# One joint inverse for the blocks of four heads, a pool of SBUF for the opening, and modulation's products joined by fours and by twos

## The chip, the cores and the metric

The kernel runs on one core of a Trainium2 chip. The metric is device time in microseconds (us), as the median of three runs. The engines are named as the profile names them: PE is TensorE, PEld its weight loads, DVE is VectorE, ACT is ScalarE, POOL is GpSimd and SP is SyncE, which here issues all DMAs. Matrix products of the type float32r (here two halves of a float32, high and low) pass the array once, products of plain float32 are recorded as two instructions each.

## The reference

The reference is a decoder trunk of two layers on 256 tokens of width 2048, in float32. Each layer computes

```
mod = silu(c) @ w_ada[l] + b_ada[l]        # 2048 x 12288; six vectors: shift, scale, gate, twice
h = rms_norm(x) * (1 + scale) + shift
proj = h @ w_in[l]                         # q,k,v,z of 8 DeltaNet heads, 16 query heads, 2 k, 2 v
x = x + gate * (concat(deltanet, attention) @ w_out[l])
h = rms_norm(x) * (1 + scale') + shift'
x = x + gate' * ((silu(h @ w_gate) * (h @ w_up)) @ w_down)
```

For this change the DeltaNet head matters. After a causal convolution of four taps and a silu, q and k are normalised; per head there is a matrix of scores of k against k with a decay, and the reference solves with its lower triangle:

```
lower = where(strict, (k beta) k^T * decay, 0) + eye
t_inv = triangular_solve(lower, eye)       # the inverse, per chunk of 64 tokens
w, u = t_inv @ (k beta exp(g)), t_inv @ (v beta)
```

## The kernel before

The program is written through a planner. Each piece of work is a Python generator that yields the engine of its next step; a class `Timed` keeps a clock of estimated costs for each engine, and `Steps` lets a piece go on when that clock says that its input is there. So the order of instructions on each engine is fixed when the program is built; on the chip, semaphores hold each instruction until its input is there. All DMAs stand in one order on SP, and a DMA that waits for a free buffer holds those behind it.

The program runs in these stages: an **opening**, the rest of layer 0's **heads** stage, layer 0's **FFN** stage, layer 1's heads stage, layer 1's FFN stage. In the FFN stages and in the projections, each weight block of 128x128 is split by ACT and DVE (or POOL) into a high half `wh` and a low half `wl`; for one block PE computes `wh` with both halves of the activation `act` and `wl` with its high half. In the heads stages these are three products of 256 columns, in the FFN stages one of 512 columns and one of 256. Weights come in loads of 512 KB through 4 buffers `w`.

In the opening, w_ada for two of the six vectors of layer 0 (64 loads of 512 KB, tile `wada`, 3 buffers, class `Ada`) is multiplied on PE (`products`): one load gives four matmuls of 32x256 in plain float32, which stand in the four column groups of the array. Another 64 such loads follow in layer 0's heads stage; all other w_ada rows go to DVE. As soon as columns of the modulation are there, the activations `hs` are made one after another, and 28 of the 42 column tiles of w_in (`EARLY`) are multiplied in groups of k (`GROUPS`), the last of which, k from 10 on, begins the heads stage.

The list `JOBS` sets the order of the 42 projections: for head after head k, q, one pair of attention queries (aq), v, z. `delta` is one DeltaNet head from k and q to its output. It computes the matrix `B` of scores, then inverts the diagonal blocks of 16x16 of its triangle, one head at a time: DVE masks and sums the blocks into `mc` (128x2x16), spreads them into `R` (128x512), PE multiplies `R` by a 0/1 matrix (`same`), and on DVE 30 instructions of multiply and sum (`jk`, `uc`) make one column after another. From these blocks, `U` (and its transpose `W`), PE and DVE build the inverse of 128x128 in steps of 16, 32 and 64, and then the output. Before the projection v of head h, the planner waits until `delta` of head h-2 has passed the point "mid".

The main loop projects in the order of `JOBS`; `split_act` takes one of 38 buffers `act`. The wait before v reads `while h > 1 and "mid" not in sts[h - 2]: S.wait()`.

Of the kernel before, what the change touches and what calls it, by code (L numbers as in the profile page):

```python
# [21 lines left out]
F32R = mybir.dt.float32r  # L22
# [7 lines left out]
EPS = 1e-6  # L30
NACT = 38
# [3 lines left out]
AHEAD = 2  # L35
# [25 lines left out]
for _n, _w in (  # L61
    ("ident", 128), ("triX", 256), ("sel", 8), ("ls", 128), ("amask", 256), ("cos", 256), ("sin", 256),
    ("own", 128), ("same", 128), ("id16", 16), ("nid16", 16), ("bm", 8), ("m16", 8),
):
    CONST.add(_n, _w)
# [7 lines left out]
def constants():  # L73
# [10 lines left out]
    out["own"], out["same"], out["bm"] = b16 & (p < j), b16, b16[:, ::16]  # L84
    out["id16"] = p % 16 == np.arange(16)[None, :]
    out["nid16"] = -1.0 * out["id16"]
# [9 lines left out]
class Timed:  # L96
# [13 lines left out]
    def dma(self, out, in_, after=0):  # L110
# [6 lines left out]
        return self.loads + 2000  # L117

# [55 lines left out]
HEADS = {"pm": 3, "psm": 5}  # L174
FFN = {"pr": 2, "psm": 4}


class Build:


    def __init__(self, nc, sb, tc):
        self.nc, self.sb, self.tc = nc, sb, tc
        self.k = self.stage = 0
        self.ps = None
        self.free = {"act": NACT, "cv": 4, "w3": 5, "do": 2, "th": 2, "dn": 2, "ry": 2, "kq": 3, "z": 3, "n2": 6}
# [3 lines left out]
    def banks(self, tags):  # L189

        if self.ps is not None:
            for tag in self.tags:
                assert self.free.pop(tag) == self.total.pop(tag), tag
            self.ps.__exit__(None, None, None)
        self.tags = tags
        if tags:
            self.ps = self.tc.tile_pool(name=f"ps{self.stage}", bufs=1, space=PSUM)
            self.pool = self.ps.__enter__()
            self.stage += 1
            self.free.update(tags)  # L200
            self.total.update(tags)
# [11 lines left out]
    def t(self, tag, shape, dt=F32, bufs=None):  # L213
        self.k += 1
        return self.sb.tile(shape, dt, tag=tag, name=f"{tag}_{self.k}", bufs=self.total.get(tag, bufs))
# [78 lines left out]
class Weights:  # L294
# [6 lines left out]
    def __init__(self, b):  # L301
# [3 lines left out]
        self.tiles, self.freed, self.ready, self.cur = {}, {}, {}, []  # L305

# [23 lines left out]

    def load(self, upto):
        while self.loaded < min(upto, len(self.units), self.loaded - len(self.tiles) + self.BUFS):
            u = self.loaded
            src, n = self.units[u]
            w = self.b.t("w", [128, 1024], bufs=self.BUFS)
# [3 lines left out]
            self.tiles[u] = (w, self.nc.dma(to, src, self.freed.get(u - self.BUFS, 0)))  # L339
# [50 lines left out]
def trunk(tc, xT, bada, c, c_col, par, con, w_in, w_ba, w_ada0, w_ada, w_out, w_gu, w_dn, out):  # L390
    nc = Timed(tc.nc)
    with (
# [4 lines left out]
        b.banks(HEADS)  # L397
# [65 lines left out]
        class Ada:  # L463
            BUFS = 3

            def __init__(self):

                self.todo = [(0, m, j, i) for j in range(8) for m in (1, 0) for i in range(4)]
                self.todo += [(0, m, j, i) for m in COLS[2:] for j in range(8) for i in range(4)]
# [23 lines left out]

            def load(self):
                l, m, k, i = self.todo[self.nload]
                w = b.t("wada", [128, 1024], bufs=self.BUFS)
# [4 lines left out]
                self.tiles[self.nload] = (w, nc.dma(w, src, self.freed.get(self.nload - self.BUFS, 0)))  # L501
                self.nload += 1

            def products(self):
# [3 lines left out]
                for n in range(self.cols):  # L508
# [94 lines left out]
            def loads(self, u):  # L603
                n = min(max(self.want(u + 3), self.force), len(self.todo))
                while self.nload < n and self.nload - self.ndone < self.BUFS:
                    self.load()
# [33 lines left out]
        def pump():  # L640
            while first:
                kind, n = first[0]
                if kind == 0 and ada.nload - ada.ndone < ada.BUFS:
                    ada.load()
                elif kind == 1 and len(W.tiles) < W.BUFS:
# [84 lines left out]
        def act_tile():  # L730
            return b.t("act", [128, 2, T], F32R)

        def split_act(src, outs, at):
            yield from b.take("act", A_)
            a = act_tile()
# [897 lines left out]
```

## Time and profile before

| what | value |
|---|---|
| median of three runs | 2598.65 us |
| fastest and slowest of the three | 2586.24 and 2600.52 us |
| profiled execution, its own time | 2599.8 us |
| its span from first to last instruction | 2598.1 us |
| mean granted TensorE clock | 0.988 |
| busy share of the span: PE, DVE, ACT, POOL | 96%, 73%, 50%, 17% |
| DMA, mean over the span | 234 GB/s |

The time outside the span is 1.7 us. In the page, a group's row gives engine, operation, the tile that is written and the tiles that are read, the shape, the count, the busy time in us, the mean of one in ns, and after the second bar the idle time just before these instructions and what ended it. All rows have the line of the recording helper (L161, and L116 for DMAs), so tiles tell the groups apart.

### The profile page before, as it was taken

The numbers are of one execution on the slowest core, as the hardware profiler recorded it, in microseconds if no ns is written. First come the engines' busy times: TensorE is split into PE (matmuls) and PEld (weight loads), VectorE is DVE, ScalarE is ACT, GpSimd is POOL, SyncE is SP. The second block draws the span as 40 slices with busy tenths as digits, with TensorE's granted clock in tenths as the row PEclk, the third lists the DMA queues.
The fourth block names the chain that finished last, engine by engine and source line by source line (L and its number), as shares of the span: only waits on it lengthen the run. The fifth ranks groups of instructions, "written<-read, shape, count | busy, mean of one in ns | idle before, by whom it ended". The sixth has DMA issues, their size and how long they took to land.

```text
span 2598.1 us, 46969 instructions
## 1 busy us (share of the span) xinstructions
PE 2494.3 (96%) x16910; PEld 2165.7 (83%) x16910; DVE 1905.9 (73%) x4750; ACT 1293.2 (50%) x2760; POOL 440.6 (17%) x391
## 2 busy tenths in 40 slices
PE   6999999898999999999998999999899999999998
PEld 4776777787888888888888898999788888888887
DVE  3656776998777899999997767785877655555565
ACT  3335554335455444555445655544555544555553
POOL 1323333571000000000004434346000000000000
PEclk9999999999999999999998999999999999999999
DMA  8998565686777999999993333356677766555564
GB/s 292 314 331 273 183 209 174 212 294 197 247 256 254 322 346 358 351 352 351 333 334 124 117 121 123 122 171 215 214 258 245 241 187 185 187 189 186 181 187 136
DMA packets 184092, 608.68 MB, mean 234 GB/s; under 512 B 19121, under 2 KB 30513, under 8 KB 183857
## 3 DMA queue, kind: packets, MB, share of 16 engines
q1 hardware_dynamic: 183858, 605.68, 68.8%
q8 instruction: 132, 2.16, 0.3%
q14 instruction: 102, 0.84, 0.1%
HBM read 603.51 MB, written 2.10 MB: 233 GB/s over the span
## 4 chain that ended last, share of the span: by engine, by line
PE 50%; issue 31%; DVE 10%; DMA 5%; ACT 1%; POOL 0%; SPq 0%; DVEq 0%; POOLq 0%; ACTq 0%
PE psm L161 19%; PE pr L161 17%; PE pm L161 14%; DMA wada<-w_ada 5%; DVE wl L161 2%; DVE wada L161 1%; DVE cv L161 1%; ACT wh L161 1%; DVE jk L161 1%; DVE x L161 1%; DVE U L161 0%; DVE R L161 0%; DVE act L161 0%; DVE mc L161 0%; SPq L116 0%
## 5 line engine op out<-in xcount | busy, mean ns | idle before, releaser
L161 ACT CAST wh<-w 128x512 fp32r<-128x512 f32 (+1 forms) x1566 | 913.4, 605 | 471.0 <-PE psm L161 177.0
L161 DVE TENSOR_TENSOR wl<-w,wh 128x512 fp32r<-128x512 f32 (+1 forms) x1301 | 873.0, 687 | 250.7 <-ACT wh L161 240.0
L161 PE MATMUL pr<-act,wh 128*128 128x512 f32 x2816 | 991.5, 397 | 7.3 <-DVE kq L161 4.0
L161 PE MATMUL pr<-act,wl 128*128 128x256 f32 x2816 | 790.2, 281 | 0.0
L161 PE MATMUL pm<-act,wh 128*128 128x256 f32 x3328 | 654.2, 295 | 14.6 <-DVE z L161 5.1
L161 PEld LDWEIGHTS pr<-act,wh 128*128 128x128 f32 x2816 | 530.9, 189 | 135.5 <-DVE act L161 4.7
L161 POOL TENSOR_TENSOR wl<-w,wh 128x512 fp32r<-128x512 f32 (+1 forms) x265 | 366.3, 1390 | 1247.5 <-ACT wh L161 1166.6
L161 PE MATMUL psm<-act,wh 128*128 128x512 f32 (+1 forms) x1792 | 571.9, 375 | 3.2 <-DVE act L161 2.9
L161 PEld LDWEIGHTS pm<-act,wh 128*128 128x128 f32 x3328 | 523.2, 194 | 57.7 <-issue 35.4
L161 PEld LDWEIGHTS pr<-act,wl 128*128 128x128 f32 x2816 | 533.9, 190 | 0.0
L161 PE MATMUL pm<-act,wl 128*128 128x256 f32 x1664 | 473.7, 285 | 0.0
L161 PE MATMUL psm<-act,wl 128*128 128x256 f32 x1600 | 449.0, 281 | 0.0
L161 DVE CUSTOM_DVE_ANT_0 wada<-wada,cs 128x1024 f32<-128x1024 f32 x256 | 329.0, 1286 | 97.4 <-DMA wada<-w_ada 97.0
L161 PEld LDWEIGHTS psm<-act,wh 128*128 128x128 f32 x1792 | 325.0, 189 | 81.0 <-issue 10.7
L161 PEld LDWEIGHTS pm<-act,wl 128*128 128x128 f32 x1664 | 321.8, 193 | 0.0
L161 PEld LDWEIGHTS psm<-act,wl 128*128 128x128 f32 x1600 | 303.5, 190 | 0.0
L161 ACT COPY kq<-pr 128x512 f32<-128x512 f32 x88 | 51.6, 587 | 179.5 <-PE pr L161 179.4
L161 POOL TENSOR_TENSOR n2r<-ms,halfc 128x2 f32<-128x2 f32 x5 | 3.4, 689 | 810.5 <-DVE ms L161 810.5
L161 DVE TENSOR_TENSOR kq<-pr,kq 128x512 f32<-128x512 f32 x88 | 60.5, 688 | 75.7 <-ACT kq L161 75.7
L161 PE MATMUL psm<-wada,cs 128*32 128x256 f32 x1024 | 87.6, 416 | 28.3 <-DMA wada<-w_ada 28.1
L161 DVE SCALAR_TENSOR_TENSOR x<-psm,mod,x 128x256 f32<-128x256 f32 x128 | 61.9, 483 | 62.7 <-PE psm L161 60.3
L161 ACT ACTIVATE th<-kq 128x256 f32<-128x256 f32 x88 | 36.8, 418 | 76.4 <-DVE kq L161 76.4
(176 smaller groups left out, 1723.9 us busy)
## 6 DMA issues: line engine op xcount, KB each, us to landing
wada<-w_ada SPq DMA_DIRECT2D x384, 512.0 KB, 5.8
w<-w_gu SPq DMA_DIRECT2D x352, 512.0 KB, 4.9
w<-w_in SPq DMA_DIRECT2D x147, 512.0 KB, 3.8
w<-w_dn SPq DMA_DIRECT2D x128, 512.0 KB, 4.6
w<-w_out SPq DMA_DIRECT2D x64, 512.0 KB, 3.8
w<-w_dn SPq DMA_DIRECT2D x64, 384.0 KB, 4.4
w<-w_in SPq DMA_DIRECT2D x28, 384.0 KB, 4.7
x<-xT SPq DMA_DIRECT2D x4, 512.0 KB, 7.6
```

The source lines that it names most:

```text
L161: return f(*a, **k)
```

## The change

The inverses of the 16x16 blocks are made for four heads at once. `delta` is cut in two: `scores` goes as far as `mc` of its head; when four heads are there, `inverses` runs once. It carries `mc` by eight small DMAs (8 KB each) into `qi`, where one partition holds a whole 16x16 block, so that the inverse is made along the free dimension: blocks of 2, then 4, 8 and 16 with 18 to 20 DVE instructions on 64 partitions for all four heads. Eight more DMAs carry the result back into `uc`. The 0/1 product and `R` of before are gone, and so are the 30 instructions per head. `delta` then starts from `uc`; the transposes of v move from its start to after the inverse, and "mid" with them; the sum of squares of q moves into `scores`.

`JOBS` now has k and q of heads 0 to 3 first, then v, z of head h with k, q, aq of head h+4 behind them.

SBUF gets pools by stage. The opening has its own: 8 buffers `wx` for the first 64 loads of w_ada instead of 3, and 4 buffers `wy` for every second load of w_in beside the 4 of `w`. The heads stages get `B` six times instead of twice in the freed room; 8 of the 38 `act` buffers become `mid`, for the FFN stage alone.

`products` now waits until four loads (the first 64) or two loads (the later 64) are there and multiplies them one after the other.

```diff
-NACT = 38
+NACT, NMID = 30, 8
...
+AHEAD, BATCH = 2, 4
 JOBS = [("ak", 0), ("av", 0)] + [("aq", h) for h in range(AHEAD)]
+for _h in range(BATCH):
+    JOBS += [("k", _h), ("q", _h)] + [("aq", AHEAD + _h // 2)] * (_h % 2)
 for _h in range(H):
-    JOBS += [("k", _h), ("q", _h)] + [("aq", _h + AHEAD)] * (_h + AHEAD < H) + [("v", _h), ("z", _h)]
+    JOBS += [("v", _h), ("z", _h)]
+    for _n in range(BATCH, H):
+        if _n - BATCH == _h:
+            JOBS += [("k", _n), ("q", _n), ("aq", _n)]
...
+    def carry(self, out, in_):
+
+        self.nc.sync.dma_start(out=out, in_=in_)
+        self.count += 1
+        self.end = max(self.end, self.floor)
...
-HEADS = {"pm": 3, "psm": 5}
-FFN = {"pr": 2, "psm": 4}
+JOIN = 4, 2
+
+
+HEADS = {"pm": 3, "psm": 5}, {"w3": 5, "B": 6, "z": 3, "dn": 2, "ry": 2}
+FFN = {"pr": 2, "psm": 4}, {"mid": NMID}
+
+START = HEADS[0], {"ry": 1, "wx": 8}
...
+    def tag(self, u):
+
+        return "wy" if u < self.marks["mix0"] and u % 2 else "w"
...
-                w = b.t("wada", [128, 1024], bufs=self.BUFS)
+                early = self.nload < self.first
+                w = b.t("wx" if early else "wada", [128, 1024], bufs=self.BUFS)
...
-                    while n not in self.tiles or self.tiles[n][1] > S.now() or self.busy[half] and begin:
-                        yield N_
-                    yield P_
+                    join = JOIN[n >= self.first]
+                    if n % join == 0:
+                        while (
+                            any(n + d not in self.tiles or self.tiles[n + d][1] > S.now() for d in range(join))
+                            or self.busy[half] and begin
+                        ):
+                            yield N_
+                        yield P_
...
+            st.update(B=B, qn=qn, rk=rk)
+            bt["n"] += 1
+            if bt["n"] == BATCH:
+                S.add(inverses(bt, bt["ui"]), 0)
+
+        def inverses(bt, ui):
+
+            yield A_
+            qi = b.t("qi", [64, 272], bufs=1)
+            for x_ in range(2 * BATCH):
+                nc.carry(
+                    out=qi[x_ * 8 : x_ * 8 + 8, 0:256].rearrange("m (i j) -> m i j", j=16),
+                    in_=bt["mc"][:, x_ // 2, x_ % 2, :],
+                )
+            nc.end += 7500
+            yield D_
...
+            for n in (4, 8):
...
+                for out, lhs, rhs in ((half, qn_(0, 1), un_(1, 1)), (un_(0, 1), un_(0, 0), half)):
                     yield D_
-            b.give("psm")
+                    for x_ in range(t):
+                        nc.vector.tensor_tensor(
+                            out=tmp[:, x_], in0=lhs[:, x_].unsqueeze(2).to_broadcast([64, n, n, n]),
+                            in1=rhs[:, x_].rearrange("p k j -> p j k").unsqueeze(1).to_broadcast([64, n, n, n]), op=ALU.mult,
+                        )
+                        nc.vector.tensor_reduce(out=out[:, x_], in_=tmp[:, x_], op=ALU.add, axis=mybir.AxisListType.X)
+            yield A_
+            uc = b.t("uc", [128, BATCH, 2, 16], bufs=2)
+            for x_ in range(2 * BATCH):
+                nc.carry(
+                    out=uc[:, x_ // 2, x_ % 2, :],
+                    in_=ui[x_ * 8 : x_ * 8 + 8, 0:256].rearrange("m (i j) -> m i j", j=16),
+                )
+            nc.end += 7500
+            yield N_
+            bt["uc"] = uc
+
+        def delta(l, h, st, bt, y16, outs):
+
+            while "uc" not in bt:
+                yield N_
+            yield from b.take("head", D_)
...
-            yield from b.take("psm", P_)
-            q = b.bank()
-            nc.tensor.matmul(q, C("same"), R.rearrange("p c k -> p (c k)"), start=True, stop=True)
-            qk = q.rearrange("p (a c k) -> p a c k", a=2, c=16)
...
-            for c in range(1, 16):
-                for blk in range(2):
-                    junk = b.t("jk", [128, 16], bufs=2)
-                    nc.vector.tensor_tensor_reduce(
...
+            while "v" not in st:
+                yield N_
+            yield from b.take("psm", P_)
+            q = b.bank()
+            for tb in range(2):
+                nc.tensor.transpose(q[:, tb * 128 : tb * 128 + 128], st["v"][:, tb * 128 : tb * 128 + 128], ident)
+            st["mid"] = True
...
+                elif kind == "v":
+                    S.add(delta(l, h, sts[h], bts[h // BATCH], y16s[h % 2], outs), 0)
+                    while h > 1 and "mid" not in sts[h - 2]:
+                        S.wait()
```

On all of PE, 512 products of w_ada stand in 120 places between float32r products before and in 46 places in the change; 16 products with `R` are gone, and no other product of PE is added or removed. DVE has 927 instructions fewer, SP 64 DMAs more. Three places follow.

PE in the opening. `psm_98` and `psm_111` collect the products of w_ada (`wada`, `wx` are loads, `cs` holds silu(c)); `act` with `wh` and `wl` are float32r products of w_in. Before:

```order
L161 MATMUL psm_797<-act_532,wl_685 128x256
L161 MATMUL psm_98<-wada_682,cs_66 32x256 x4
L161 MATMUL psm_797<-act_580,wh_684 128x256 x2
L161 MATMUL psm_797<-act_580,wl_685 128x256
L161 MATMUL psm_817<-act_532,wh_684 128x256 x2
L161 MATMUL psm_817<-act_532,wl_685 128x256
L161 MATMUL psm_98<-wada_720,cs_66 32x256 x4
L161 MATMUL psm_827<-con_64,th_818 128x1 x2
```

And in the change:

```order
L172 MATMUL psm_452<-act_246,wl_340 128x256
L172 MATMUL psm_111<-wx_202,cs_69 32x256 x4
L172 MATMUL psm_111<-wx_206,cs_69 32x256 x4
L172 MATMUL psm_111<-wx_210,cs_69 32x256 x4
L172 MATMUL psm_111<-wx_214,cs_69 32x256 x4
L172 MATMUL psm_452<-act_263,wh_339 128x256 x2
L172 MATMUL psm_452<-act_263,wl_340 128x256
```

Four loads that stood alone between float32r products stand behind one another.

SP in layer 1, around the second joint inverse (heads 4 to 7). `qi` and `uc` are the small DMAs, `w` are loads of w_in; the brackets give the semaphores that SP waits for, DMAHW those of earlier DMAs on the same one of eight semaphores:

```order
L126 DMA qi_19936<-mc_18168 8x16x16 [waits DMAHW1_49,DVE_49]
L126 DMA qi_19936<-mc_18168 8x16x16 [waits DMAHW2_49]
L121 DMA w_19955<-w_in 128x1024 [waits DMAHW3_49,DVE_49,Pool_49]
L121 DMA w_20007<-w_in 128x1024 [waits DMAHW4_49,DVE_49,Pool_49]
L121 DMA w_20054<-w_in 128x1024 [waits DMAHW5_49,DVE_49,Pool_49]
L121 DMA w_20109<-w_in 128x1024 [waits DMAHW6_49,DVE_49]
L121 DMA w_20163<-w_in 128x1024 [waits DMAHW3_49,DMAHW7_49,DVE_49,Pool_49]
L121 DMA w_20223<-w_in 128x1024 [waits DMAHW0_49,DMAHW4_49,DVE_49,Pool_49]
L126 DMA uc_20225<-ui_16394 128x1x16 [waits DMAHW1_49]
```

Six weight loads, each waiting for its buffer, stand between the way out and the way back; before there were weight loads alone.

PE in layer 1, where the blocks of heads 4 and 5 are used (`U_20305`, `U_20308`; `vT` is v of head 4). The last rows ahead of v of head 6:

```order
L172 MATMUL pm_20201<-act_16371,wh_20154 128x256 x2
L172 MATMUL pm_20201<-act_16371,wl_20155 128x256
L172 MATMUL psm_20311<-con_67,U_20305 128x128 x2
L172 MATMUL psm_20314<-con_67,U_20308 128x128 x2
L172 MATMUL psm_20322<-W_20317,B_18116 128x64 x2
L172 MATMUL psm_20325<-W_20319,B_18759 128x64 x2
```

From here to `psm_20398<-con_67,vT_19876` there are 31 more rows, that one included, without any float32r product, all steps of the two heads' inverses; before, a head's steps stood between float32r products, as here the removed one does:

```order
L161 MATMUL pm_21561<-act_16585,wl_21456 128x256
L161 MATMUL psm_21604<-dy_21516,B_21046 128x128 x3
L161 MATMUL psm_21608<-R_21582,con_64 128x512
L161 MATMUL pm_21561<-act_16606,wh_21455 128x256 x2
L161 MATMUL pm_21561<-act_16606,wl_21456 128x256
```

More of the change, by code (lines that the diff above doesn't have):

```diff
@@ L1322, in delta @@
                 )
-            for tb in range(2):
-                nc.tensor.matmul(q[:, 256 + tb : 257 + tb], sq[:, tb * 128 : tb * 128 + 128], one, start=True, stop=True)
-            b.give("cv")
             yield D_
@@ L1429, in delta @@
             b.give("psm")
+            b.give("B")
             b.give("head")
```

247 lines of the change are left out of this document (143 added, 104 removed).

## The prediction

> **What bounds the kernel now.** I read the page's first part, then the stages by windows, then PE's rows in order of time, then PE's waits. By the page PE is the bound:
>
> ```profile
> span 2598.1 us, 46969 instructions
> PE 2494.3 (96%) x16910; PEld 2165.7 (83%) x16910; DVE 1905.9 (73%) x4750; ACT 1293.2 (50%) x2760; POOL 440.6 (17%) x391
> ```
>
> By stages (us; busy time and instructions of each engine; granted clock, DMA share, GB/s):
>
> ```profile
> 0.00:34.00 34.00, 14.43 (x90) 6.03 (x90) 8.83 (x21) 8.69 (x17) 2.94 (x8) 1.00 0.83 279
> 34.00:191.00 157.00, 154.29 (x1353) 121.26 (x1353) 88.32 (x192) 59.27 (x123) 49.09 (x38) 1.00 0.92 318
> 191.00:498.00 307.00, 286.01 (x2479) 224.41 (x2479) 229.07 (x1000) 160.80 (x453) 106.61 (x113) 0.98 0.64 213
> 618.00:1364.00 746.00, 737.92 (x4226) 646.92 (x4225) 646.45 (x1230) 377.88 (x708) 2.58 (x2) 0.99 0.88 313
> 1368.00:1738.00 370.00, 353.20 (x2908) 326.16 (x2908) 279.85 (x1103) 209.55 (x547) 156.97 (x147) 0.98 0.39 128
> 1826.00:2598.00 772.00, 753.25 (x4244) 652.19 (x4244) 492.79 (x875) 387.10 (x723) 1.38 (x2) 0.99 0.62 199
> ```
>
> The change leaves the two FFN stages (746 and 772 us) as they are. What it can move lies in the other 1080 us: the opening to 191 us, layer 0's heads up to 618, layer 1's from 1364 to 1826. PE is busy nearly throughout there too (154 of 157 us, 353 of 370), and a busy PE may still stream badly, so the next rows look at single instructions. A gain has to come from PE work that goes away, or from the few per cent in which PE waits. DVE has slack (280 of 370 us): work taken from it is worth only what PE waits for it.
>
> **The change, part by part.** *The product with R goes.* PE in order of time (start, length):
>
> ```profile
> 379.46 0.28 PE L161 MATMUL pm<-act,wl 128*128 128x256 f32 x1
> 379.58 1.02 PE L161 MATMUL psm<-R,con 128*128 128x512 f32 x2
> 380.04 0.80 PE L161 MATMUL pm<-act,wh 128*128 128x256 f32 x2
> 380.67 0.28 PE L161 MATMUL pm<-act,wl 128*128 128x256 f32 x1
> 381.03 0.28 PE L161 MATMUL pm<-act,wl 128*128 128x256 f32 x1
> ```
>
> From wl to wl, three float32r products, it is 0.36 us without it (380.67 to 381.03), so 0.12 us for each, and 1.21 with it (379.46 to 380.67): 0.85 us, though the records overlap. 16 x 0.85 = **-13.6**. This term is sure; nothing on PE takes its place.
>
> *Products of w_ada are joined.* PE in the opening:
>
> ```profile
> 87.16 0.40 PE L161 MATMUL psm<-act,wh 128*128 128x256 f32 x2
> 87.40 0.28 PE L161 MATMUL psm<-act,wl 128*128 128x256 f32 x1
> 87.61 0.64 PE L161 MATMUL psm<-wada,cs 128*32 128x256 f32 x8
> 88.18 0.50 PE L161 MATMUL psm<-act,wh 128*128 128x256 f32 x2
> ```
>
> The wl at 87.40 would be followed at 87.52, and the next float32r product starts at 88.18: a load that stands alone costs PE 0.66 us. A further load in a group costs at least what 256 columns of float32 stream, half of the 0.85 above, 0.43, and at most 0.66. No row shows two loads back to back on a warm PE; I take 0.48, nearer to streaming, since the gap before (0.09) and part of the 0.57 from 87.61 to 88.18 belong to the change of form. Saved per joined load: 0.18 (0 to 0.23). The opening joins 48 of 64 loads (three of each four), layer 0's heads 32 of 64: 48 x 0.18 = 8.6 and 32 x 0.18 = **-5.8** (0 to -11.0, 0 to -7.4).
> The Trainium skill, TensorEngine Tiling (Array Packing), Key Properties, says that a change of the tiling mode drains TensorE and a change of tile within the mode does not. By that a joined load costs the streaming alone, and the two terms would be 11.0 and 7.4, the sum 4 us lower. The row above agrees as far as it shows a cost beside the streaming.
>
> *Eight load buffers more.* Ahead of the first float32r product PE waits for loads and single steps:
>
> ```profile
> 31.61 1.08 PE L161 MATMUL psm<-wada,cs 128*32 128x256 f32 x8
> 34.12 1.10 PE L161 MATMUL pm<-act,wh 128*128 128x256 f32 x2 [1.43 <-ACT act L161]
> ```
>
> And SP, in the first 230 us, waits mostly for PE to free a buffer (total, times, longest):
>
> ```profile
> SPq L116 <- PE psm L161: 105.0, 71, 5.1
> ```
>
> With 8 buffers the first eight loads stream in without waiting for PE, the last product ahead of the first `hs` comes earlier; I take 4 us (0 to 8). How far the opening can shrink is set by DMA: until 191 us it moved 34 x 279 + 157 x 318 KB, 59.4 MB; at a full share that is 318 / 0.92 = 346 GB/s, 172 us, and some 3 us to start. So 16 us at most. Joining (8.6) and the earlier start (4) give 12.6; I take **-12** (-16 to +6; the 6 if PE stands at groups of four that lack their last load).
>
> *Waits of PE that go.* PE's waits in layer 0 from 191 to 498 us:
>
> ```profile
> PE psm L161 <- DMA wada<-w_ada: 9.6, 10, 2.7
> PE pm L161 <- DVE z L161: 5.1, 1, 5.1
> PE psm L161 <- DVE R L161: 1.6, 2, 1.2
> ```
>
> and in layer 1 from 1368 to 1738:
>
> ```profile
> PE psm L161 <- DVE R L161: 5.5, 6, 1.2
> PE psm L161 <- DVE vT L161: 4.7, 5, 2.1
> ```
>
> The waits for R have no successor on PE, and the transposes of v, which now stand after the inverse, find v made: 11.8 us, of which a part will come back at the next instruction in PE's order; I take **-8** (0 to -12). The waits for w_ada I leave as they are: half as many, but each for the later of two loads.
>
> *DVE.* In layer 1's 370 us (busy, mean ns, idle before):
>
> ```profile
> L161 DVE CUSTOM_DVE_ANT_0 jk<-uc,psm 128x2 f32<-128x2 f32 (+14 forms) x240 | 27.4, 162 | 1.1
> L161 DVE DVE_READ_ACCUMULATOR2_ANT uc<- 128x1 f32 x240 | 19.8, 83 | 0.5 <-issue 0.5
> L161 DVE TENSOR_TENSOR R<-mc,con 128x512 f32<-128x512 f32 x8 | 6.0, 749 | 0.3
> ```
>
> Some 35 to 50 us per layer go (the first two overlap); two joint inverses come back, each with four instructions of R's size (0.75) and some 14 small ones (0.16 to 0.25), about 6 us. PE sees of that the one long wait for z, a gate that DVE made late: **-3** (0 to -5).
>
> *The joint inverse's way adds waits.* Scores to mc, at layer 1's last head, on PE and on DVE:
>
> ```profile
> 1716.12 1.53 PE L161 MATMUL psm<-kq 128*128 128x512 f32 x4 [0.62 <-DVE kq L161]
> ```
> ```profile
> 1720.37 0.60 DVE L161 TENSOR_REDUCE mc<-do 128x32 f32<-128x256 f32 x1
> ```
>
> From 1716.12 to 1720.97 are 4.9 us. No row shows a DMA of 8 KB landing; SP starts two small ones 0.46 us apart, and the nearest rows of landing (last number, us) are
>
> ```profile
> 1.24 0.42 SPq L116 DMA_DIRECT2D mod<-bada  x1
> 1.70 0.42 SPq L116 DMA_DIRECT2D par<-par  x1
> ```
> ```profile
> w<-w_in SPq DMA_DIRECT2D x147, 512.0 KB, 3.8
> mod<-bada SPq DMA_DIRECT2D x1, 96.0 KB, 2.1
> ```
>
> On the way out only the last head's two carries are late: 0.5 + 2.1, about 3 us. On the way back the last carry waits for the weight load issued just ahead to land: 3.8 + 2.1, about 6 us (4 to 8). With 4.9 to mc and some 7 on DVE among its other work, 21 us pass from a batch's last scores to `U`. Where PE has float32r work for that long, it costs nothing: in layer 1's first batch eleven projections of 48 products, 11 x 48 x 0.12 = 63 us, lie between the last q and v of head 2. In its second batch PE's order has 195 float32r products (23 us) and some 3 us of attention from head 7's scores to `U`: just covered; but the way back stands on SP behind a load whose buffer, that of four loads earlier, comes free only some 40 products (5 us) before `U`, against the carries' 6: 1 to 3 us are left. Then come the 35 rows without a float32r product, two heads by turns between PE, DVE and ACT, and v of head 6 behind them. Before, one head's same steps took from here to here:
>
> ```profile
> 1731.02 0.38 PE L161 MATMUL psm<-con,U 128*128 128x128 f32 x2
> ...
> 1745.81 0.44 PE L161 MATMUL psm<-U,yn 64*64 64x64 f32 x4
> ```
>
> 15 us with other work in between. With nothing in between and two heads filling each other's gaps I take 8, half of it PE work that was needed anyway. Layer 0's second batch has the same rows; in its first the projections left are short (k from 10 on alone), and one stretch of PE's order is as bare. I take 6 + 5 + 4 = **+15** for the three places (+5 if the steps hide each other, +45 if each place costs the whole 15).
>
> *The rest.* 30 `act` buffers hold the 16 of `hs` and 14 others, more than are in use before `hs` is freed; `mid` is used as those 8 were: nothing.
>
> **The sum:** -13.6 - 5.8 - 12 - 8 - 3 + 15 = -27.4 against the profiled execution's 2599.8 (1.7 of it outside the span): 2572. The three runs' median lies 1.2 lower, so I say **2571** us; the forecast's own terms let it lie between 2558 and 2584.
>
> **The rivals.**
> (a) *The new waits hide*: SP and DVE run ahead, two heads fill each other's gaps, DMA fills the opening. -13.6 - 7.4 - 16 - 12 - 5 + 5 = -49: 2550. For it: PE's waits in the rows above are short. Against it: the 35 rows stand alone in PE's order.
> (b) *PE only changes what it waits for*: joining saves nothing, the waits for R and v come back elsewhere, the opening gains only its start. -13.6 - 4 - 3 + 15 = -6: 2593. For it: the DMA share of 0.92 leaves the opening little room. Against it: the 0.66 us.
> (c) *The round trip is too long, and the kernel gets slower.* The carries, 8 KB in 128 pieces of 64 bytes, could land one after another, 8 x 2.1 = 17 us each way. Then 4.9 + 17 + 7 + 17 = 46 us stand against the 26 of cover in layer 1's second batch: 20 us of wait there and about as much at the two places of layer 0, on top of the 15; and DVE, where `U` stands in order ahead of the splits, would hold up the weights. -42 + 15 + 60 = +33: 2632. From about 10 us each way the gain is gone. Against it: eight semaphores let eight DMAs run at once.
> The Trainium skill, DMA: Bandwidth & Descriptors, Rules for kernel authors, says to coalesce small transfers, as under 64 KB one pays mostly overhead. Each carry is an eighth of that, so by the page (c) is what the eight of a way would pay for. No row here shows a row of such DMAs.
>
> **Chances and range.** The forecast 0.5, (a) 0.22, (b) 0.17, (c) 0.11. About 0.5% (13 us) is what can be told from no change. Faster: the forecast and (a), 0.72; the same: (b), 0.17; slower: (c), 0.11. The range of 8 in 10 leaves out a tenth below (a) and (c) above: 2545 to 2601.
>
> **What would show it.** Right: no rows of R; products of w_ada in groups of 32 and 16 records with 0.43 to 0.48 us per further load; the first float32r product before 31 us and k from 10 on by 180; layer 1's heads stage 5 to 15 us shorter, with waits of 4 to 8 us in all ahead of v of head 6. Wrong: PE or DVE waiting over 10 us for qi or uc; an opening as long as before at a DMA share of 0.92; weight loads late behind the carries.

## The result and the profile after

The changed kernel takes 2571.36 us (median of 5 runs, 2569.78 to 2576.98) against 2594.06 for the kernel before in the same comparison (5 runs, 2586.24 to 2600.52): a ratio of 0.9913, 95% interval 0.9891 to 0.9935. The forecast was 2571. The time came out, but the terms said -27.4 us and the change is -22.7 here; the forecast was taken from a median before of 2598.65. Of nine executions of a kernel below, "opening and joining alone", one took 12613 us, and that kernel's ratio leaves it out.

The first part of the page of the changed kernel:

```profile
span 2569.6 us, 46036 instructions
PE 2462.8 (96%) x16878; PEld 2174.5 (85%) x16878; DVE 1854.1 (72%) x3823; ACT 1294.3 (50%) x2760; POOL 432.7 (17%) x389
```

To see where the time went I cut both traces at the same counts of float32r products of PE. The change reorders these within the heads stages, but the number in each stage stays: k from 10 on begins (product 840), the FFN of layer 0 begins (2784), layer 1's heads begin (7008), its FFN begins (9792). By these windows, first the kernel before (length, then busy time and instructions of PE, PEld, DVE, ACT, POOL, then granted clock, DMA share, GB/s):

```profile
0.00:190.90 190.90, 168.62 (x1442) 127.19 (x1442) 97.05 (x213) 67.96 (x138) 52.03 (x46) 1.00 0.91 311
190.90:619.70 428.80, 391.82 (x3341) 325.19 (x3337) 337.95 (x1241) 210.74 (x565) 177.77 (x158) 0.98 0.66 224
619.70:1368.50 748.80, 739.71 (x4234) 648.18 (x4234) 646.48 (x1232) 379.15 (x710) 3.27 (x3) 0.99 0.88 312
1368.50:1833.90 465.40, 443.71 (x3665) 414.93 (x3665) 335.56 (x1204) 251.64 (x633) 206.81 (x183) 0.98 0.44 144
1833.90:2598.10 764.20, 750.44 (x4234) 650.16 (x4234) 488.84 (x864) 383.67 (x717) 0.69 (x1) 0.99 0.62 200
```

and the changed kernel:

```profile
0.00:175.70 175.70, 152.59 (x1443) 128.88 (x1443) 97.39 (x209) 65.74 (x136) 53.89 (x47) 0.98 0.94 338
175.70:591.30 415.60, 380.28 (x3325) 327.48 (x3321) 313.67 (x775) 213.37 (x569) 181.94 (x162) 0.96 0.68 231
591.30:1347.10 755.80, 748.10 (x4234) 653.89 (x4234) 646.39 (x1232) 379.69 (x710) 3.27 (x3) 0.99 0.87 309
1347.10:1809.30 462.20, 435.24 (x3649) 411.19 (x3649) 308.99 (x746) 252.29 (x633) 192.92 (x177) 0.97 0.44 146
1809.30:2569.60 760.30, 746.60 (x4234) 653.08 (x4234) 487.69 (x864) 383.21 (x717) 0.69 (x1) 0.99 0.62 201
```

The opening lost 15.2 us, layer 0's heads 13.2, layer 1's heads only 3.2. The FFN of layer 0, whose products the change leaves as they are, grew by 7.0, and that of layer 1 shrank by 3.9. In both heads stages the granted clock fell, from 0.98 to 0.96 and 0.97. Three questions follow: which edits made the gain, why layer 1 gained so little, and what the FFN's 7 us are.

**A group of four loads** in the opening, PE in order of time:

```profile
85.23 0.29 PE L172 MATMUL pm<-act,wl 128*128 128x256 f32 x1
85.44 1.93 PE L172 MATMUL psm<-wx,cs 128*32 128x256 f32 x32
87.31 0.50 PE L172 MATMUL pm<-act,wh 128*128 128x256 f32 x2
```

The float32r product due at 85.35 starts at 87.31: 1.96 us for four loads, where one alone cost 0.66 before. A further load costs (1.96 - 0.66) / 3 = 0.43 us, so joining saves 0.22 per load and not 0.18. In layer 0's heads a pair of loads between float32r products costs 1.09 us (median), by the same price. The Trainium skill, TensorEngine Tiling (Array Packing), Key Properties, has a change of tile within one mode free of the drain; the trace agrees, since the 0.43 are the streaming alone.

**The second joint inverse of layer 1.** SP, in order of time:

```profile
1626.38 5.33 SPq L126 DMA_DIRECT2D qi<-mc  x8
1631.83 16.03 SPq L121 DMA_DIRECT2D w<-w_in  x6
1647.90 5.26 SPq L126 DMA_DIRECT2D uc<-ui  x8
1653.28 0.39 SPq L121 DMA_DIRECT2D w<-w_in  x1
1653.71 0.43 SPq L121 DMA_DIRECT2D wada<-w_ada  x1
```

DVE:

```profile
1627.70 0.61 DVE L172 TENSOR_REDUCE mc<-do 128x32 f32<-128x256 f32 x1
...
1633.98 1.08 DVE L172 COPY ui<-qi 64x8 f32<-64x8 f32 x2
...
1645.52 0.68 DVE L172 TENSOR_REDUCE ui<-R 64x64 f32<-64x512 f32 x1
...
1651.40 0.90 DVE L172 TENSOR_TENSOR U<-uc,con 128x128 f32<-128x128 f32 x4 [0.24 <-DMA uc<-ui]
1658.86 1.23 DVE L172 CUSTOM_DVE_ANT_0 wada<-wada,cs 128x1024 f32<-128x1024 f32 x1 [6.56 <-DMA wada<-w_ada]
1660.01 0.08 DVE L172 DVE_READ_ACCUMULATOR2_ANT n<- 128x1 f32 x1
1660.01 0.48 DVE L172 TENSOR_TENSOR y<-psm,con 128x128 f32<-128x128 f32 x2
```

and PE:

```profile
1621.53 1.45 PE L172 MATMUL psm<-kq 128*128 128x512 f32 x4
```
```profile
1649.49 0.28 PE L172 MATMUL pm<-act,wl 128*128 128x256 f32 x1
1651.75 0.94 PE L172 MATMUL psm<-con,U 128*128 128x128 f32 x4 [1.98 <-DVE U L172]
1652.74 1.23 PE L172 MATMUL psm<-W,B 128*128 128x64 f32 x8
1660.35 0.69 PE L172 MATMUL psm<-y,U 128*128 128x64 f32 x2 [6.38 <-DVE y L172]
```

From the last scores (1621.5) to `mc` (1628.3) are 6.8 us, to the first use of `qi` 5.7, through DVE's inverse 12.2, back to `U` 5.2: 29.9 us, where I had 21. The cover was longer too, so PE waits 1.98 us for `U`, inside the 1 to 3 foretold. The dear wait is the next one. DVE's order has a product of modulation ahead of `y`; its load of `w_ada` stands on SP behind the eight carries, which hold SP until 1653.2, and lands only for 1658.9. DVE waits 6.56 us for it, PE 6.38 for `y`.

### The profile page after: what moved, and what is told of

It is laid out like the page before. It is cut to its first block, busy times and chain, and to the rows that moved or that the text cites. A ratio compares the mean times of both kernels' runs of the same rounds, so it can differ in the third digit from the quotient of the medians.

```text
span 2569.6 us, 46036 instructions
## 1 busy us (share of the span) xinstructions
PE 2462.8 (96%) x16878; PEld 2174.5 (85%) x16878; DVE 1854.1 (72%) x3823; ACT 1294.3 (50%) x2760; POOL 432.7 (17%) x389
## 4 chain that ended last, share of the span: by engine, by line
PE 52%; issue 32%; DVE 9%; DMA 3%; ACT 2%; POOL 1%; SPq 1%; DVEq 0%; POOLq 0%; ACTq 0%
PE psm L172 19%; PE pr L172 18%; PE pm L172 15%; DMA wada<-w_ada 3%; DVE wl L172 2%; ACT wh L172 1%; DVE wada L172 1%; POOL wl L172 1%; DVE act L172 1%; DVE cv L172 1%; DVE R L172 1%; DVE x L172 1%; DMA wx<-w_ada 0%; SPq L121 0%; DVE ry L172 0%
## 5 line engine op out<-in xcount | busy, mean ns | idle before, releaser
L172 ACT CAST wh<-w 128x512 fp32r<-128x512 f32 x1532 | 894.2, 604 | 456.7 <-PE psm L172 177.0
L172 PE MATMUL pm<-act,wh 128*128 128x256 f32 x3328 | 641.4, 292 | 14.0 <-DVE x L172 4.1
L172 PEld LDWEIGHTS pm<-act,wh 128*128 128x128 f32 x3328 | 519.0, 192 | 36.3 <-issue 21.2
L172 POOL TENSOR_TENSOR wl<-w,wh 128x512 fp32r<-128x512 f32 (+1 forms) x239 | 331.0, 1395 | 1190.9 <-PE psm L172 762.5
L172 PE MATMUL psm<-act,wh 128*128 128x512 f32 (+1 forms) x1280 | 390.8, 362 | 2.4 <-DVE act L172 2.1
L172 PE MATMUL psm<-act,wl 128*128 128x256 f32 x1088 | 308.3, 283 | 0.0
L172 PEld LDWEIGHTS psm<-act,wh 128*128 128x128 f32 x1280 | 228.3, 189 | 46.0 <-issue 6.1
L172 PEld LDWEIGHTS psm<-act,wl 128*128 128x128 f32 x1088 | 205.2, 189 | 0.0
L172 PE MATMUL psm<-mid,wh 128*128 128x512 f32 x512 | 183.4, 396 | 0.0
L172 PE MATMUL psm<-mid,wl 128*128 128x256 f32 x512 | 144.1, 281 | 0.0
L172 PEld LDWEIGHTS psm<-mid,wh 128*128 128x128 f32 x512 | 96.1, 188 | 22.8
```

Source lines behind the costliest of these rows:

```text
L172: return f(*a, **k)
```

## The experiments

The stage lengths below are cut at the same float32r products, from one profile of each kernel; "opening" ends where k from 10 on begins. The times are medians, the ratios against the kernel before in the same comparison, which stood between 2596.57 and 2598.0 (23, 25 and 14 runs in the three comparisons); the row of the change is from the comparison above. "Before, again" is one execution.

| kernel | time us, ratio (95%) | opening | layer 0 heads | FFN 0 | layer 1 heads | FFN 1, end |
|---|---|---|---|---|---|---|
| before | | 190.9 | 428.8 | 748.8 | 465.4 | 764.2 |
| before, again | 2597.9 | 188.7 | 422.8 | 756.9 | 462.9 | 764.9 |
| the change | 2571.4, 0.9913 (0.9891 to 0.9935) | 175.7 | 415.6 | 755.8 | 462.2 | 760.3 |
| single loads | 2596.4, 1.0017 (0.9995 to 1.0039) | 187.6 | 432.3 | 756.2 | 462.2 | 757.8 |
| old opening | 2598.7, 1.0015 (0.9997 to 1.0034) | 189.8 | 433.3 | 757.1 | 461.5 | 759.4 |
| single loads in the heads | 2594.5, 0.9979 (0.9958 to 1.0000) | 174.8 | 433.4 | 757.4 | 462.2 | 760.5 |
| joint inverse alone | 2597.0, 1.0000 (0.9980 to 1.0020) | 189.5 | 431.4 | 751.6 | 462.1 | 756.8 |
| opening and joining alone | 2576.3, 0.9924 (0.9897 to 0.9950) | 175.4 | 416.8 | 755.1 | 460.5 | 760.9 |
| the product twice | 2594.9, 1.0009 (0.9977 to 1.0041) | 189.4 | 428.0 | 760.8 | 465.1 | 765.4 |
| carries counted | 2575.4, 0.9925 (0.9902 to 0.9947) | 175.0 | 423.1 | 760.9 | 456.1 | 760.6 |
| earlier k and q | 2559.0, 0.9865 (0.9841 to 0.9890) | 174.8 | 415.9 | 754.7 | 448.9 | 761.3 |
| earlier still | 2561.3, 0.9886 (0.9852 to 0.9920) | 175.7 | 411.2 | 753.6 | 455.3 | 763.0 |
| earlier k and q, carries counted | 2561.1, 0.9876 (0.9839 to 0.9913) | 174.6 | 413.1 | 760.8 | 447.7 | 762.6 |

### Which edits made the gain

**Single loads.** `JOIN = 4, 2` becomes `JOIN = 1, 1`.

> The changed kernel with each load of w_ada multiplied by itself again (1 and 1 in place of 4 and 2); buffers, pools and the joint inverse stay. By the prediction's terms this gives back 48 x 0.18 + 32 x 0.18 = 14 us; by the changed kernel's trace, where a group of four loads takes PE 1.96 us and one alone 0.66, a joined load saves 0.22 and 80 of them 18 us: 2585 to 2589 us, and k from 10 on begins at 184 to 187 us in place of 175.7. If PE only changes what it waits for (rival b), the opening stays at 176 us, and the time at 2571.

2596.4 us, and the whole gain is gone: 25 us, more than the 14 to 18 of PE time. The opening gives back 11.9 us, as joining's price says (48 x 0.22 = 10.6); layer 0's heads give back 16.7.

**The old opening**, with loads by twos kept in the heads:

```diff
-JOIN = 4, 2
+JOIN = 1, 2
-START = HEADS[0], {"ry": 1, "wx": 8}
+START = HEADS[0], {"ry": 1, "wx": 3}
-        return "wy" if u < self.marks["mix0"] and u % 2 else "w"
+        return "w"
```

> The changed kernel with the opening of before: three buffers for w_ada and four for the weights, each load by itself until k from 10 on; layer 0's heads keep the loads by twos, and the joint inverse stays. If the opening's 15.2 us are joining and buffers together, k from 10 on begins at about 191 us again and the time is 2586. Beside the kernel with single loads and all buffers, the difference between the two openings is what the buffers are worth: 2 to 5 us if joining carries the opening (my terms: 4), 10 or more if the buffers do, because loads then run ahead of PE.

The opening is 189.8 us. Against single loads with all buffers (187.6) the buffers alone are worth 2.2 us, no more than two profiles of the kernel before differ by (190.9 and 188.7), and against the change joining by fours is worth 11.9: joining carries the opening. But the time is 2598.7 and not 2586: layer 0's heads take 433.3, as long as with single loads, though their loads go by twos.

**Single loads in the heads only**: `JOIN = 4, 1`.

> The changed kernel with the opening's loads of w_ada still by fours, but layer 0's heads multiplying each of theirs by itself (4 and 1 in place of 4 and 2). A joined load saves 0.22 us of PE by the changed kernel's trace: 32 x 0.22 = 7 us, 2578 us, and k from 10 on still begins at 176. If joining in the heads does more than save PE time (both kernels before it, one with single loads there and one with loads by twos but a late opening, took 17 us longer from there to the FFN), it is 2584 to 2589. If it saves nothing there, 2571.

The opening stays at 174.8, and layer 0's heads take 433.4, 17.8 more than by twos, where 7 are PE time. Neither of my prices explains that, so the inverse was tried by itself.

**The joint inverse alone**: the three lines of the old opening, and `JOIN = 1, 1`.

> The joint inverse alone: the changed kernel with single loads of w_ada, three buffers for them and four for the weights in the opening, so that only the product with R, the waits for R and v, DVE's share and the new waits are left of the change. By the prediction's terms -13.6 - 8 - 3 + 15 = -10 against before: 2584 to 2588 us. By the two kernels that undid joining or the opening and stood at 2596 and 2599, what is left brings nothing or a loss: 2596 to 2610 us, with the second batches' rows and TensorE's half clock behind them in the place of the gain.

The time of before, 1.0000 (0.9980 to 1.0020). Layer 1's heads are no more than 3.3 us shorter than before, layer 0's 2.6 to 8.6 longer than in the two profiles of before. In layer 0 the granted clock shows a part of why:

```profile
189.50:620.90 431.40, 395.15 (x3322) 332.06 (x3320) 317.47 (x773) 213.47 (x566) 178.99 (x159) 0.94 0.65 223
```

0.94 against 0.98: over some 430 us the clock was at half for (0.98 - 0.94) x 430 / 0.5, some 30 us more than before. The other two kernels with single loads there have 0.94 as well, the old opening 0.93, the change 0.96.

**The opening and the joining alone**: the changed kernel with each head's own `delta`, the product with `R`, two buffers `B`, the old `JOBS` and the old loop over heads.

> The opening and the joining alone: the changed kernel with each head's own inverse, the product with R and the order of heads of before; loads of w_ada by fours in the opening and by twos behind it, eight buffers and four more for the weights there. The joint inverse alone stood at 1.000 of before. If the parts add up, all of the change's 25 us are here: 2570 to 2575 us, 14 of them until k from 10 on and about 10 in layer 0's heads. If joining in the heads only gives back what the joint inverse had cost there (17 us between the kernels with and without it), it is worth its PE time here, 32 x 0.22 = 7 us, and the time is 2575 to 2580 or a little more. If the inverse carries a part of the gain, 2583 or more.

0.9924 (0.9897 to 0.9950), beside 0.9913 of the whole change: nearly all of its gain. Layer 0's heads, by the window,

```profile
175.40:592.20 416.80, 383.80 (x3340) 326.35 (x3336) 345.82 (x1240) 212.15 (x569) 182.69 (x162) 0.98 0.70 230
```

are 6 to 12 us shorter than before at the same clock of 0.98, of which joining's PE time is 7.0. So opening and joining together bring about 20 of the change's 23 us, and the joint inverse nothing that can be told from zero, with them or without them.

But beside the joint inverse the two don't simply add: fours in the opening alone stand at 0.9979, twos in the heads alone at 1.0015, both at 0.9913. Layer 0's heads take 431 to 433 us in all four kernels that leave out either. In this table PE's idle time is the length less PE's busy time, and the time at half clock is added up from each trace's record of the granted clock, which is either 1 or 0.5:

| kernel | layer 0 heads, us | PE idle | at half clock |
|---|---|---|---|
| before; again | 428.8; 422.8 | 37.0; 33.5 | 16.8; 13.5 |
| the change | 415.6 | 35.3 | 36.8 |
| single loads in the heads | 433.4 | 37.8 | 51.9 |
| old opening | 433.3 | 39.2 | 64.6 |
| joint inverse alone | 431.4 | 36.3 | 48.0 |
| opening and joining alone | 416.8 | 33.0 | 14.1 |

The window of the old opening:

```profile
189.80:623.10 433.30, 394.06 (x3338) 338.30 (x3336) 317.06 (x776) 213.57 (x567) 179.62 (x158) 0.93 0.66 223
```

At half clock a float32r product takes 0.213 us (three in the change's trace, 1670.86 to 1671.50) in place of 0.12, so a microsecond there costs at most some 0.44 us (an estimate). Against the change, single loads in the heads have 7 us more PE work, 2.5 more idle time and 15.1 more at half clock, at most 6.6: some 16 of the 17.8. The old opening has hardly more PE work there, but 3.9 more idle time and 27.8 more at half clock, at most 12: some 16 of the 17.7. So what single loads seemed to cost beside PE time is not theirs alone. The planner's order of the stage shifts with each of these edits; which of its choices bring the half clock isn't shown, and without the joint inverse only the two together were run.

### What the product with R was worth

**The product twice**, in the kernel before, with nothing else moved:

```diff
             nc.tensor.matmul(q, C("same"), R.rearrange("p c k -> p (c k)"), start=True, stop=True)
+            nc.nc.tensor.matmul(q, C("same"), R.rearrange("p c k -> p (c k)"), start=True, stop=True)
```

> The kernel before with the product with R issued twice into the same bank, and nothing else moved: what 16 such products cost. By the prediction's first term, 0.85 us each and nothing that hides them: +13.6 us, 2608 to 2612 beside 2596. If PE waits there anyway (for DVE, for a load), they cost less: +3 to +8 us.

1.0009 (0.9977 to 1.0041): -6 to +11 us; 13.6 lies outside. PE in order of time shows that the second product does take its time (L1253 is its line):

```profile
1446.94 1.10 PE L161 MATMUL psm<-R,con 128*128 128x512 f32 x2 [0.23 <-DVE R L161]
1447.88 1.02 PE L1253 MATMUL psm<-R,con 128*128 128x512 f32 x2
1448.34 0.80 PE L161 MATMUL pm<-act,wh 128*128 128x256 f32 x2
1448.97 0.28 PE L161 MATMUL pm<-act,wl 128*128 128x256 f32 x1
```

From the first product's start to the next wl are 2.03 us; in the prediction's rows, with one product, 1.09 (379.58 to 380.67). So the second costs 0.94 on the spot. Yet layer 1's heads take 465.1 us with eight of them, 465.4 and 462.9 without; layer 0's 428.0, against 428.8 and 422.8. One place where it is taken back can be seen: PE's waits for `vT` in layer 1's heads were 4.7 us in five, and are

```profile
PE psm L161 <- DVE vT L161: 3.5, 2, 2.1
```

More of it shows in what PE does not lose: in the two heads stages together PE is idle for 50.8 us with the second products, 58.7 and 56.0 in the two profiles without, and the clock is at half for 20.8 us, against 38.4 and 25.8. How much of that the products cause isn't shown; two profiles of the same kernel differ as much (422.8 and 428.8 in layer 0). Nor was the product taken away by itself.

### Why the joint inverse brought nothing

**Carries counted.** The planner is told that a carry takes SP's time, so that it places work on what is loaded behind the carries later:

```diff
     def carry(self, out, in_):
+        self.loads = max(self.loads, self.clock["tensor"], self.floor) + 650
         self.nc.sync.dma_start(out=out, in_=in_)
```

> The changed kernel, whose planner now counts 0.65 us on SP for each carry, so that it takes what is loaded behind the carries to arrive later and places the work on it later. In the changed kernel's trace a load of w_ada is issued at 1653.7 us right behind eight carries of U, DVE waits 6.56 us for it at 1658.9, and y, which stands behind on DVE, holds PE for 6.4 us. If the carries' time on SP is the cause, this wait goes and those for w_ada and c behind layer 0's carries shrink: 5 to 10 us, 2561 to 2566. If the bare rows between PE, DVE and ACT are what costs there, PE waits as long for the next of them, and the time stays within 3 us of 2571.

The wait for `y` is gone. PE's waits in layer 1 around the second inverse (total, times, longest), first in the change:

```profile
PE psm L172 <- DVE y L172: 6.4, 1, 6.4
PE psm L172 <- DVE U L172: 2.0, 1, 2.0
```

then with the carries counted:

```profile
PE psm L173 <- DVE U L173: 2.4, 2, 1.9
PE psm L173 <- DVE yn L173: 1.4, 1, 1.4
```

So the cause of the 6.4 us is shown, and layer 1's heads are 6.1 us shorter. Layer 0's are 7.5 longer: in the planner's new order there PE is idle for some 3 us more, and the clock is at half for 14 us more (0.94 in place of 0.96). The time stays where it was. The wait was real, and repairing it alone brought nothing that shows.

**Earlier k and q.** The scores of the second batch are moved away from their first use:

```diff
-    for _n in range(BATCH, H):
-        if _n - BATCH == _h:
-            JOBS += [("k", _n), ("q", _n), ("aq", _n)]
+    for _n in ((4,), (5, 6), (7,), ())[_h] if _h < 4 else ():
+        JOBS += [("k", _n), ("q", _n)]
+    for _n in ((), (), (4, 5), (6, 7))[_h] if _h < 4 else ():
+        JOBS += [("aq", _n)]
```

> The changed kernel with k and q of heads 5 to 7 projected one place earlier (5 and 6 behind head 1, 7 behind head 2) and the attention's q of heads 4 to 7 later (4 and 5 behind head 2, 6 and 7 behind head 3). In layer 1's order 246 float32r products now lie between the last scores and the second batch's first U, 195 before, and the four heads' rows behind it lie 90 to 100 products apart instead of two by two with none between. If the new waits come from too little cover (the prediction's +15), most of the 23 us that layer 1 loses from its 8790th to its 9024th product go, and some of layer 0's: 2550 to 2558 us. If the round trip itself is what costs (the carries and DVE's 12 us of inverse, wherever they stand), PE waits as long ahead of U, and the time stays within 4 us of 2571.

2559.0 us, 0.9865 (0.9841 to 0.9890), 1 us past the expected range: faster than both kernels, with layer 1's heads 13.3 us shorter than in the change and all other stages the same. Between 1650 and 1675 us, where both kernels work on the second batch, the change has

```profile
1650.00:1675.00 25.00, 16.02 (x126) 14.60 (x127) 8.76 (x31) 4.87 (x16) 1.27 (x1) 0.59 0.23 73
```

and this kernel

```profile
1650.00:1675.00 25.00, 24.49 (x223) 23.17 (x221) 13.79 (x38) 12.82 (x35) 9.39 (x8) 1.00 0.53 166
```

PE is busy throughout, and at full clock. In the change PE waits for 9 of the 25 us, and the clock of 0.59 means half speed for (1 - 0.59) x 25 / 0.5 = 20.5 us. Cut where the clock falls:

```profile
1650.20:1653.60 3.40, 1.80 (x12) 1.42 (x12) 1.85 (x6) 0.93 (x3) 0.00 (x0) 1.00 0.26 47
1653.60:1674.10 20.50, 13.32 (x109) 12.28 (x108) 6.34 (x22) 3.74 (x12) 1.27 (x1) 0.50 0.23 77
```

It falls before the wait for `y` begins (1653.97), behind the 1.98 us for `U` and the first small products. With the carries counted that wait is gone, and the clock falls at nearly the same place of the order all the same:

```profile
1659.70:1663.10 3.40, 1.40 (x10) 0.93 (x8) 2.66 (x7) 1.28 (x4) 0.00 (x0) 1.00 0.52 143
1663.10:1680.20 17.10, 14.58 (x114) 13.70 (x115) 7.02 (x24) 4.40 (x14) 1.26 (x1) 0.50 0.30 94
```

So the wait for `U` and the bare rows are enough for the half clock, and the long wait isn't needed. What it costs is less than its 20.5 us: PE works for 13.3 of them, some 6 us lost by the 0.44 above (an estimate). In all of layer 1's heads PE is idle for 7.3 us less with k and q earlier (19.7 for 27.0). The two together come to the 13.3 us.

SP's carries take as long as before (5.34 and 5.80 us for eight); what changed is that float32r products lie between the rows. The only wait left there is

```profile
PE psm L173 <- DVE y L173: 0.5, 1, 0.5
```

The order moves two things at once, more products ahead of the first `U` and products between the four heads' rows, and no run takes them apart; nor was this order tried without the joint inverse.

The Trainium skill, TensorE: Matmul & The Clock Gate, Part 1, has the clock go to half after an idle window of about 3.4 us and back after a busy one. The traces here show half clock without such an idle window: it falls behind 3.4 us in which PE worked for 1.8 and 1.4, with no wait longer than 1.98, and stays down while PE runs the bare rows, small products with pauses between them.

**Earlier still**: k and q of head 4 ahead of the first v, of 5 behind head 0, of 6 and 7 behind head 1.

> The kernel with k and q of heads 5 to 7 earlier (2559 us), and these and head 4's one place earlier still: k and q of head 4 ahead of the first v, of 5 behind head 0, of 6 and 7 behind head 1. Layer 1's second batch then has 363 float32r products between its last scores and its first U in place of 246, and layer 0's 222 in place of 138. If cover still lacks in layer 0 (its TensorE clock is at half for 13.7 us from 297 us and 6.8 from 390 us there), 4 to 10 us more are gained: 2549 to 2555. If layer 1's 246 were enough and layer 0's first batch is as bare as before (its first two U stand at one place in the order still), it is 2556 to 2562.

2561.3 us, 0.9886 (0.9852 to 0.9920): no different from the kernel above by these intervals. Layer 0's heads are 4.7 us shorter, layer 1's 6.4 longer.

**Both the order and the carries counted.**

> The kernel with k and q of heads 5 to 7 earlier, whose planner also counts 0.65 us on SP for each carry. With the cover, no load behind carries held PE in layer 1 any more, so there is nothing to gain there: 2556 to 2562 us. In layer 0 one wait of 3.9 us for w_ada is left behind the carries: if the planner now sees it, 2553 to 2557.

2561.1 us, 0.9876 (0.9839 to 0.9913), the same again. Once the bare rows have cover, counting the carries makes no difference that shows.

### What the FFN's 7 us are

**The kernel before once more**, for a second profile.

> The kernel before once more, unchanged, for a second profile of it: how long a pair of float32r products takes in each FFN stage. In the first profile it was 347 ns in layer 0's and 353 in layer 1's, in the changed kernel 351 in both, which makes its FFN stage 7 us longer in layer 0 and 4 shorter in layer 1. If the rate belongs to the kernel, 347 and 353 come again; if it is set anew in each execution, other values between 346 and 358 come.

In layer 0's FFN PE streams pairs of float32r products, one of 512 columns and one of 256, a record each. Two windows of the first profile of before:

```profile
660.00:840.00 180.00, 180.00 (x1041) 157.43 (x1040) 130.49 (x237) 93.16 (x178) 0.00 (x0) 1.00 0.74 250
```
```profile
1000.00:1200.00 200.00, 200.00 (x1155) 176.34 (x1154) 185.08 (x351) 104.80 (x197) 0.00 (x0) 1.00 0.97 351
```

and of the second:

```profile
660.00:840.00 180.00, 180.00 (x1021) 156.09 (x1020) 125.14 (x227) 90.33 (x174) 0.00 (x0) 1.00 0.72 244
```
```profile
1000.00:1200.00 200.00, 200.00 (x1156) 176.34 (x1155) 184.96 (x350) 104.94 (x198) 0.00 (x0) 1.00 0.97 351
```

A pair took 346 ns in the first window of the first profile (180 us / 520.5) and 353 in that of the second, by the same instructions at full clock with PE busy throughout; in the second windows both took 346. In the change it was 351, here in the second window:

```profile
1000.00:1200.00 200.00, 200.00 (x1141) 175.32 (x1140) 182.44 (x347) 104.05 (x197) 0.00 (x0) 1.00 0.96 345
```

No records are missing that could feign this: the stage has 4234 and 4235 in the two profiles. With 2112 pairs a stage, 5 to 7 ns are 10 to 15 us. So neither of the two expectations holds alone: the rate differs between executions of one kernel, and within one. The FFN's +7.0 and -3.9 can therefore not be put down to the change, and single profiles should not be compared there. What sets the rate isn't settled.

## Why the prediction was right, and where it was not

**The opening, -12.** Right: -15.2 in the two profiles compared, -13.0 against the second of before, within -16 to +6. Its parts were 8.6 and 4; measured were 11.9 for joining and 2.2 for the buffers, the second no larger than chance between profiles. Joining was undersized because I took 0.48 us for a further load and it is 0.43, the lower bound; the buffers were oversized. The bound of 16, set by DMA, was nearly reached (its share rose to 0.94).

**Joining in the heads, -5.8.** The mechanism held; the size was low for the same reason (7.0 of PE time). With the joint inverse beside it, undoing it cost 17.8, of which 10 have no term in the sum: idle time and half clock, which undoing the opening brought too.

**The product with R, -13.6, "this term is sure".** This step failed. The price on PE is right (0.85 us; a second copy takes 0.94), but 16 more of them cost -6 to +11 us. I counted an instruction's time on PE as time of the kernel because PE was busy 96%, although the same sum had PE waiting for DVE in these stages; time that is saved ahead of such a wait can lengthen the wait. That this is where all of it went is argued: the waits for `vT` and less idle time and half clock show pieces of it.

**The waits for R and v, -8, and DVE, -3.** No run takes them apart. With the product and the new waits they made -13.6 - 8 - 3 + 15 = -9.6 for the joint inverse; by itself it measured 0 (-5 to +5).

**The new waits, +15.** The mechanism was right, its size was not. For layer 1's second batch I had 6, the round trip and the bare rows; giving it cover brought 13.3. The round trip was foretold well enough in what it leaves PE to wait (1.98 us), though by two errors that met: 29.9 us in place of 21, with more cover. What I had missed was SP's eight carries holding the next load of `w_ada` back, which stood on the list of what would make the prediction wrong as weight loads late behind the carries, and TensorE's half clock on the bare rows, which stood nowhere. The forecast sign that layer 1's heads would be 5 to 15 us shorter did not come either: they are 3.2 and, against the second profile of before, 0.7 shorter.

**The sum.** That 2571 came out within 1 us is luck. The terms say -27.4 us, and the change measured -22.7 (-17 to -28 by its interval). The time met the forecast all the same because the sum was taken from the 2598.65 of three runs, and the five runs of the comparison have 2594.06. Of the terms, the joint inverse's 9.6 too many stand against some 2 us that opening and joining brought beyond their 17.8 (20, with 13 to 27 in its interval).

**The rivals.** (a) had the better terms for the opening (-16) and for joining (-7.4), and the worse ones for the rest. (b) was wrong on joining. (c) did not come: the first use of `qi` follows the end of its carries' issue (1631.71) by 2.3 us, so they do not land one after another. DVE was held up, as (c) has it, but by a load of `w_ada` late behind the carries.

## What to carry to other kernels

An instruction of a busy engine need not be worth its length: 16 copies of a product of 0.85 us cost less than 13.6 us here. Issue it twice before removing it, and see what that costs. Work that is moved into one joint step needs its cover beside it: the same joint inverse was worth 0, and the kernel 12 us more once its inputs were made earlier and float32r products lay between its rows. On SP, which works in order, eight small transfers held back every load behind them for 5 to 6 us, and a planner that doesn't count this puts work on those loads too early; here that was one wait of 6.4 us, and counting it left the time where it was. And where edits shift a planner's whole order, their gains need not add: fours in the opening and twos in the heads gave 5 us and nothing one at a time beside the joint inverse, and 23 us together.

## What the runs showed of the hardware

TensorE's granted clock is 1 or 0.5 in these traces, and a short wait with bare rows brings it to half: it fell behind 3.4 us in which PE worked for 1.8 and 1.4, and stayed down for 20.5 and 17.1 us, the second with no wait longer than 1.9. A float32r product of 256 columns then took 0.213 us in place of 0.12. An 8 KB carry in 64-byte pieces holds SP for 0.6 us, more than a 512 KB load (0.33 to 0.43), and eight of them hold it for 5.3 to 6.1. A long run of equal pairs of float32r products streams at one of several steady rates (346, 351 and 353 ns a pair were seen), which differ between executions of one kernel and within one; a stage of 750 us moves by 10 us with that.
